# A streaming encoder layer on one core: buffers, lags, the queue of FFN weights, and the framework's scheduling model

## The chip, the cores and the metric

The kernel runs on one core of a Trainium2 chip. Time is device time in microseconds (us); lower is better. A core has a matrix engine (TensorE, in profiles PE, with its weight loads as PEld), a vector engine (VectorE, DVE), a scalar engine (ScalarE, ACT), a general one (GpSimd, POOL) and a queue engine (SyncE, SP), which here only issues DMA transfers. Each engine works through its own list of instructions in order; semaphores make one engine wait for another. SBUF is the on-chip memory, PSUM holds the results of matmuls, in 8 banks.

## The reference

One layer of a hybrid encoder over 2,048 prompt frames and 64 sample frames, width 1024. Shortened to what is computed:

```python
h = rms_norm(x, norm1_g) * (1 + sc1) + sh1            # sc, sh, gt: from silu(c) @ w_ada + b_ada
glu_a, glu_b, q, k, v, g_conv, g_attn = split(h @ w_in)
u = glu_a * sigmoid(glu_b)
conv_out = silu(layer_norm(depthwise_conv31(u))) @ w_conv_out
q, k = rms_norm per head (8 heads of 64)
o = softmax(q k^T / 8 + rel_bias, over own chunk of 64 and the 8 before) @ v
merged = sigmoid(g_conv) * conv_out + sigmoid(g_attn) * (o @ w_attn_out)
x = x + gt1 * (merged @ w_o)
h2 = rms_norm(x, norm2_g) * (1 + sc2) + sh2
gate, up = split(h2 @ w_ffn_in)                        # 2 x 2816 columns
x = x + gt2 * ((silu(gate) * up) @ w_ffn_out)
```

The outputs are both `x`, the last convolution inputs, and the new rows of keys and values. All data is 32 bit.

## The kernel before

Each large product is made of three matmuls on split operands: a value is rounded to a high part, the rest is the low part, and `mm3` adds high x high, high x low and low x high. So each weight slab (128 x 1024) passes through a chain: a DMA brings the raw slab (tags `wst`, three buffers, `wup`, one, `wfo`, two), ACT copies it into `whi`, and POOL or DVE subtracts to make `wlo`. There are five buffers (`held`) of each. A slab that is used again is written to DRAM already split (`w_d..._h`, `_l`) and later read back by DMA alone.

The work has two stages. In the first (to about 1210 us of the profile), four blocks of some 512 frames (`PBLOCKS`) are normalised, turned to columns, and multiplied with the input projection. Beside that run the depthwise convolution on DVE (480 instructions), the layer norm, and attention by head. For a head, `load_qk` fetches `q2` and `kk` (one buffer each, four DMAs on SP); four score tiles `sc` (one buffer of two PSUM banks) go to DVE and ACT for the softmax (`pr`), are transposed by TensorE (`ptp`), split (`ph`, `pl`) and multiplied with `vv` (`po`). In the second stage, three blocks (`CBLOCKS`) each run the merge (`ps<-cin`), the output projection (`pw`), the residual with second norm and transposes (`residual`), and the FFN. The FFN uses a Strassen-like scheme on halves of the frames (operands `t1` to `t4`, `b11` to `b22`, weight sums `ws` made on POOL), and `down` multiplies pairs of hidden tiles with `w_ffn_out` (`pd`). The last `down` of a block takes four tiles at once.

The order of the work comes from two layers. The kernel's own planner, class `Stream`, keeps an estimated load of each engine, and decides while the code is emitted when a step of a lane (attention, convolution, norms, residual turns) comes up between matmuls; its lags are constants such as `TURN_LAG`, `DMA_LAG`, and its prices are in `Stream.add`. Class `Weights` decides when raw slabs are loaded, split and freed. After that the framework's scheduler (`tile.TileContext`) simulates the emitted program, puts the instructions of each engine in a final order, gives out the buffers and sets the semaphores.

The profile names line 99 for nearly all instructions, because each goes through `Meter.run`; it is read by tile names instead. The lines the change touches: `last_phase` and `free_tag` (the raw buffers a kind may use), `split` (which engine makes `wlo`), `available` (whether the next slab may be split), `first_rows`, `store_v` and `norm_tile` (the buffers of `x`), `qk_rows` (the lag before key transposes), `down` (when it takes its weights), and the call of `TileContext`.

Of the kernel before, what the change touches and what calls it, by code (L numbers as in the profile page):

```python
# [16 lines left out]
P = 128  # L17
# [25 lines left out]
TT_LESS = 9e9  # L43
PE_LAG = 400.0
TURN_LAG = 2500.0
ON_ACT = (3,)
ON_POOL = ()
DMA_LAG = 4000.0
# [108 lines left out]
class Stream:  # L157
# [7 lines left out]
    def add(self, name, op, n, args, kw):  # L165
        if name == "pe":
            x = args[1]
            if op == "transpose":
                ns = 128 / 1.2
            elif x.dtype == F32:  # L170
                ns = max(n, 64) / (2.4 if "tile_position" in kw else 0.6)
            else:
                ns = (n if n >= 256 else 512) / 2.4
        elif name == "act":
            ns = 220 + 0.83 * n
        elif name == "pool":
            ns = 180.0 * n if ALU.pow in args else 60 + 2.25 * n
        else:
            fast = op in ("tensor_scalar", "tensor_copy")
            ns = 75 + n * (8.3 if op == "reciprocal" else 0.75 if fast else 1.04)  # L180
        self.load[name] = max(self.load[name], self.load["pe"]) + ns
# [66 lines left out]
class Weights:  # L248
# [5 lines left out]
    def __init__(self, engines, pool, dram, stream, keys, source, staging, held, kept):  # L254
        self.stream = stream
        self.sync, self.act, self.dve, self.gps = engines
        self.pool, self.dram, self.keys, self.source = pool, dram, keys, source
        self.staging, self.held = staging, held
        self.sum_pool, self.sum_d, self.sums, self.hold, self.landed = None, None, {}, 0, {}
        self.room, self.leaving = {"wst": staging, "wup": 0, "wfo": 0}, {"wst": 0, "wup": 0, "wfo": 0}  # L260
        times, raws = {}, {}
        self.items, self.users, self.need, self.first, self.stored = [], [], {}, set(), {}

        def item(key):
            self.items.append(key)
            self.users.append(0)
            return len(self.items) - 1

        for i, key in enumerate(keys):
            n = times[key] = times.get(key, 0) + 1  # L270
            if key[0] == "up" and n == 1:
                self.first.add(i)
                cs = [c for f, op in key[1:] for c in self.columns_of(f, op)]
                for c in cs:
                    if c not in raws:
                        raws[c] = item(("fi", c))
                self.need[i] = sorted({raws[c] for c in cs})
                for f, op in key[1:]:
                    for c in self.parts_of(f, op):
                        self.users[raws[c]] += 1  # L280
            elif n == 1 or not kept(key):
                self.need[i] = [item(key)]
                self.users[self.need[i][0]] += 1
        self.raws = raws
        self.again = {key for key, n in times.items() if n > 1 and kept(key)}
        self.loaded, self.ready, self.used, self.freed, self.given = {}, [], 0, 0, 0

        self.extra = {"wup": 1, "wfo": 2}
        self.tags = {"fo": ("wfo",), "": ("wst", "wup")}
        self.due = {kind: [] for kind in self.tags}  # L290
        for i, key in enumerate(self.items):
            self.due[self.kind(key)].append(i)
        self.load_on("")
# [12 lines left out]

    def last_phase(self, sum_pool, sum_d):
        self.sum_pool, self.sum_d = sum_pool, sum_d
        for kind, tag in (("fo", "wfo"), ("", "wup")):
            self.room[tag] = self.extra[tag]  # L310
            self.load_on(kind)

    @staticmethod
    def kind(key):
# [1 line left out]

    def free_tag(self, kind, sure=True):

        return next((t for t in self.tags[kind] if self.room[t] + (0 if sure else self.leaving[t]) > 0), None)

    def load(self, kind, sure=True):
        tag = self.free_tag(kind, sure)
        i = self.due[kind].pop(0)
        srcs, a, b = self.source(self.items[i])
        pool, bufs = (self.pool, self.staging) if tag == "wst" else (self.sum_pool, self.extra[tag])
        st = pool.tile([P, a, b], F32, tag=tag, name=tag, bufs=bufs)
        for j, src in enumerate(srcs):
            self.sync.dma_start(st[:, j * a // len(srcs) : (j + 1) * a // len(srcs)], src)
        self.loaded[i] = st, tag
        self.room[tag] -= 1  # L330
        self.landed[i] = self.stream.load["pe"] + DMA_LAG
        if self.items[i][0] == "fi":
            self.stream.at(self.landed[i], self.presum, True)
        self.fill()

    def load_on(self, kind):
# [3 lines left out]
    def drop(self, j, name):  # L340

        self.users[j] -= 1
        if self.users[j]:
            return
        _, tag = self.loaded.pop(j)
        self.leaving[tag] += 1

        def left():
            self.leaving[tag] -= 1
            self.room[tag] += 1  # L350
            self.load_on(self.kind(self.items[j]))

        self.stream.at(self.stream.when(name), left, True)

    def operand(self, f, op):
# [6 lines left out]
        while len(made) < int(op[1]):  # L362
# [5 lines left out]
            )[j]()  # L368
            self.gps.tensor_tensor(t, x, y, e)
            made.append(t)  # L370
            for c in self.parts_of(f, f"s{j + 1}"):
                self.drop(self.raws[c], "pool")
            self.stream.at(
# [12 lines left out]
    def split(self):  # L386
# [10 lines left out]
        if not its:  # L397
            for t, d in zip((hi, lo), self.stored[key][0]):
                self.sync.dma_start(t.bitcast(F32), d)
            return  # L400
        e, name = (self.dve, "dve") if key[0] in ("in", "qkv") or key[0] == "wo" and key[1] % 2 else (self.gps, "pool")
        if i in self.first:
            parts = [(slice(4 * j, 4 * j + 4), self.operand(f, op)) for j, (f, op) in enumerate(key[1:])]
            self.stream.after("act", "pool")
# [25 lines left out]
    def available(self):  # L430
        i = len(self.ready)
        if i >= len(self.keys):
            return False
        if i in self.need:
            return self.there(i) and not (self.hold and self.keys[i][0] == "up")
        return self.keys[i] in self.stored

    def fill(self):
# [75 lines left out]
def streaming_layer(ctx: ExitStack, tc: tile.TileContext, I, O):  # L514
# [271 lines left out]
        yield  # L786

    def first_rows():
        places = ((wa, "x", 2), (wa, "x", 2), (wa, "vst", 1), (wk, "kk", 1), (wk, "q2", 1))
        return [load_x(*tl, *place) for tl, place in zip(token_tiles(*PBLOCKS[0]), places)]  # L790

    def first_block(xs):
# [99 lines left out]
        stream.at(stream.when("act", "dve"), store)  # L892

    def store_v(src, n, row):
        vst = wa.tile([P, 4, 4, HD], F32R, tag="vst", name="vst", bufs=1)
        s = src[:n].rearrange("p (a c d) -> p a c d", a=4, c=2)
        stream.after("act", "pe")
        act.activation(vst[:n, :, 0:4:3], s, AF.Copy)
        stream.after("dve", "act")
        dve.tensor_tensor(vst[:n, :, 1:3], s, vst[:n, :, 0:4:3].bitcast(F32), ALU.subtract)  # L900
        stream.at(stream.when("act", "dve"), lambda: nc.sync.dma_start(
            v_d[row : row + n].rearrange("t h d -> t (h d)"), vst[:n].rearrange("p a c d -> p (a c d)").bitcast(F32)
        ))

    def qk_rows(ps, n, g, dst, col, out_rows):
# [14 lines left out]
        if out_rows is not None:  # L920
# [1 line left out]
            e, name = either(512, TT_LESS)  # L922
            e.tensor_tensor(ko[:n], kn[:n], gk[:n].unsqueeze(1).to_broadcast([n, NH, HD]), ALU.mult)
            stream.at(stream.when(name), lambda: nc.sync.dma_start(out_rows, ko[:n].rearrange("p h d -> p (h d)")))
        yield t + TURN_LAG
        store_kq(kn.rearrange("p h d -> p (h d)"), n, dst, col, g)

    def v_rows(ps, n, t):
# [68 lines left out]
    def norm_tile(lo, t, free):  # L997

        c = slice(t - lo, t - lo + P)
        x_t = load_x(t, P, wa, "x", 2)  # L1000
        yield stream.load["pe"] + DMA_LAG
        r = square(x_t, P)
        yield stream.when("pool")
        dve.tensor_scalar(x_t, x_t, r, None, ALU.mult)
# [478 lines left out]
    turns = Lane({}, TURN_NS, wide=2)  # L1483
    stream.lanes = [turns, work]

    def drain():
        turns.drain()
        work.drain()

    W.last_phase(wk, sum_d)  # L1490

    def gt_row(w, which):
        t = quarter(f"gt{which}", 1, F32, (P, D))
# [122 lines left out]
    c0, c1 = tile_chunks(*CBLOCKS[0])  # L1616
    nxt = [first_gates, gate_columns(*c0, 1)]
    srcs = [src]
    for s, (lo, hi) in enumerate(CBLOCKS):
        tiles = token_tiles(lo, hi)  # L1620
        half = (hi - lo) // 2
# [159 lines left out]
            dve.tensor_tensor(y, y, v, ALU.mult)  # L1781
            late.append((f, 1, y))

        def down(fs):

            last = fs[-1] == NF - 1
            ws = [W.get(("fo", f)) for f in fs]
            for i, (t, n) in enumerate(tiles):
                c = slice(t - lo, t - lo + n)
                if fs[0] == 0:  # L1790
# [55 lines left out]
            turns.step(turns.gens[0])  # L1846
        W.hold = False
        W.presum()
        turns.drain()
        for step, f in ((first, 3), (first, 4), (second, 2), (second, 3), (second, 4)):  # L1850
            step(f)
            W.fill()
        for f in range(0, NF, 2):
            ops = Operands(f)
            if f // 2 % 2 and f >= NF - 4:
                hid[1] = wk.tile([P, 2, 2, CW], F32R, tag="m1", name="hid")
            up(f, ops, lambda: down([f - 2, f - 1]) if 2 <= f <= NF - 4 else None)
            up(f + 1, ops, lambda: None)
        hidden(*late.pop())
        drain()  # L1860
        gt2 = {which: gt_row(1, which) for which in {int(t < SMP) for t, _ in tiles}}
        x1s = [quarter("x1", 1, F32, (P, 3, 512)) for _ in range(4)]
        for i, (t, n) in enumerate(tiles):
# [3 lines left out]
        if s + 1 < len(CBLOCKS):  # L1867
            nxt = [gate_columns(*tile_chunks(*CBLOCKS[s + 1])[0], ct) for ct in range(2)]
            srcs = [load_mixed(*c, i) for i, c in enumerate(tile_chunks(*CBLOCKS[s + 1]))]
        down(list(range(NF - 4, NF)))  # L1870
        stream.flush()


# [27 lines left out]
```

## Time and profile before

| | us |
|---|---|
| median of 3 runs | 3077.89 (3075.58 to 3080.13) |
| profiled execution | 3072.38 |
| its span | 3070.6 |
| TensorE busy | 2960.8 (96%) |
| VectorE busy | 1781.8 (58%) |
| ScalarE busy | 1179.6 (38%) |
| GpSimd busy | 1027.6 (33%) |
| mean granted TensorE clock | 0.986 |
| data moved | 676.27 MB, 220 GB/s |

A row of a group names engine, operation, output<-inputs (buffer numbers left out) and count, then busy time and the mean duration of one in ns, then the idle time of the engine before them and what ended it. A row of waits reads: who waited <- for what: us in total, times, longest. A row of the timeline has start and length in us, engine, operation and count; in brackets stands the idle time before it. "Landing" is the time from the issue of a DMA until its data has arrived. The granted clock is the share of its full rate that TensorE was allowed.

### The profile page before, as it was taken

How to read it: one execution, taken by the hardware profiler on the slowest of the kernel's cores; microseconds unless marked ns; L12 is line 12 of the kernel's file. 1: busy time of each engine (PE TensorE's matmuls, PEld its weight loads, DVE VectorE, ACT ScalarE, POOL GpSimd, SP SyncE). 2: the span in 40 equal slices, each digit the busy share in tenths (PEclk: the TensorE clock that was granted, in tenths of full speed). 3: DMA queues.
4: the chain of work that ended last, by engine and by line, in shares of the span. 5: the costliest groups of instructions: out<-in, count | busy, mean ns of one | idle time of the engine just before them, and what ended most of it. 6: DMA issues, size and time to landing. Idle time of an engine off the chain costs nothing. (4 is left out here: it accounts for less than half of the span.)

```text
span 3070.6 us, 44482 instructions
## 1 busy us (share of the span) xinstructions
PE 2960.8 (96%) x16403; PEld 2634.3 (86%) x16403; DVE 1781.8 (58%) x3435; ACT 1179.6 (38%) x2110; POOL 1027.6 (33%) x642
## 2 busy tenths in 40 slices
PE   7899898999999999999999989999999999999999
PEld 4789776887888888898999977889999999999998
DVE  5798688677877885454444335554444556344345
ACT  3334431452254357354333332453333244322321
POOL 0201210111011102448777854344445343343331
PEclk9999999999999999999999999999999999999999
DMA  9789788887887788876455567654444965334434
GB/s 344 247 298 303 226 296 282 272 268 266 281 270 238 275 273 253 262 246 229 150 169 172 192 222 244 224 185 153 151 151 134 342 213 194 126 117 131 138 110 161
DMA packets 480167, 676.27 MB, mean 220 GB/s; under 512 B 37716, under 2 KB 316104, under 8 KB 479949
## 3 DMA queue, kind: packets, MB, share of 16 engines
q1 hardware_dynamic: 467669, 656.04, 65.2%
q10 hardware_dynamic: 12280, 17.39, 1.6%
q8 instruction: 129, 2.11, 0.3%
q14 instruction: 89, 0.73, 0.1%
HBM read 501.70 MB, written 171.61 MB: 219 GB/s over the span
## 5 line engine op out<-in xcount | busy, mean ns | idle before, releaser
L99 POOL TENSOR_TENSOR wlo<-wst,whi 128x1024 fp32r<-128x1024 f32 (+1 forms) x215 | 458.7, 2142 | 607.8 <-ACT whi L99 555.6
L99 PE MATMUL ps<-t,whi 128*128 128x352 f32 (+2 forms) x2112 | 510.4, 325 | 8.3 <-DVE t L99 3.8
L99 PE MATMUL pd<-whi,hid 128*128 128x512 f32 (+1 forms) x1496 | 467.9, 391 | 16.4 <-ACT whi L99 16.4
L99 ACT ACTIVATE whi<-wst 128x1024 fp32r<-128x1024 f32 (+1 forms) x268 | 258.9, 975 | 433.2 <-PE pd L99 180.8
L99 PE MATMUL ps<-b,whi 128*128 128x352 f32 (+2 forms) x1584 | 381.4, 324 | 2.9 <-ACT early L99 1.8
L99 PEld LDWEIGHTS ps<-t,whi 128*128 128x128 f32 x2112 | 371.1, 189 | 13.9 <-DVE t L99 5.0
L99 DVE SCALAR_TENSOR_TENSOR y<-u,wd,y 128x512 f32<-128x512 f32 (+1 forms) x480 | 369.9, 774 | 6.8
L99 PE MATMUL ps<-hh,whi 128*128 128x512 f32 (+2 forms) x992 | 364.9, 368 | 0.0
L99 PE MATMUL ps<-hl,whi 128*128 128x512 f32 (+2 forms) x992 | 347.8, 351 | 0.0
L99 PE MATMUL ps<-hh,wlo 128*128 128x512 f32 (+2 forms) x992 | 347.4, 350 | 0.0
L99 PEld LDWEIGHTS pd<-whi,hid 128*128 128x128 f32 (+1 forms) x1496 | 276.7, 185 | 79.9 <-ACT whi L99 16.8
L99 PE MATMUL ps<-t,wlo 128*128 128x352 f32 (+2 forms) x1056 | 341.9, 324 | 0.1
L99 DVE TENSOR_TENSOR acc<-acc,pd 128x512 f32<-128x512 f32 (+1 forms) x272 | 187.0, 688 | 207.5 <-PE pd L99 207.5
L99 PE MATMUL pd<-wlo,hid 128*128 128x512 f32 (+1 forms) x748 | 292.5, 391 | 2.2 <-POOL wlo L99 1.3
L99 PEld LDWEIGHTS ps<-b,whi 128*128 128x128 f32 x1584 | 276.1, 188 | 4.8 <-ACT early L99 2.7
L99 PE MATMUL ps<-b,wlo 128*128 128x352 f32 (+2 forms) x792 | 256.2, 324 | 0.0
L99 POOL TENSOR_TENSOR r<-t,mhalf 128x1 f32<-128x1 f32 (+3 forms) x68 | 83.7, 1233 | 408.9 <-DVE t L99 389.4
L99 PEld LDWEIGHTS ps<-hh,wlo 128*128 128x128 f32 x992 | 188.7, 190 | 23.5 <-issue 0.5
L99 PEld LDWEIGHTS ps<-hh,whi 128*128 128x128 f32 x992 | 189.9, 191 | 18.8 <-issue 2.5
L99 PEld LDWEIGHTS ps<-hl,whi 128*128 128x128 f32 x992 | 189.8, 191 | 15.8 <-issue 1.7
L99 PEld LDWEIGHTS ps<-t,wlo 128*128 128x128 f32 x1056 | 200.3, 190 | 0.4 <-POOL wlo L99 0.4
L99 POOL TENSOR_TENSOR wlo<-wup,whi 128x1024 fp32r<-128x1024 f32 (+1 forms) x69 | 146.0, 2116 | 149.2 <-ACT whi L99 128.8
(206 smaller groups left out, 5431.8 us busy)
## 6 DMA issues: line engine op xcount, KB each, us to landing
whi<-w_din_h SPq DMA_DIRECT2D x72, 512.0 KB, 6.2
wlo<-w_din_l SPq DMA_DIRECT2D x72, 512.0 KB, 6.6
wst<-sum_d SPq DMA_DIRECT2D x132, 256.0 KB, 2.9
wmod<-in_w_ada SPq DMA_DIRECT2D x48, 512.0 KB, 8.8
sum_d<-ws SPq DMA_DIRECT2D x88, 256.0 KB, 4.8
whi<-w_dfo_h SPq DMA_DIRECT2D x44, 512.0 KB, 5.3
wlo<-w_dfo_l SPq DMA_DIRECT2D x44, 512.0 KB, 6.5
wst<-in_w_ffn_in SPq DMA_DIRECT2D x84, 256.0 KB, 3.3
```

The lines of the kernel that those rows point to most:

```text
L99: return f(*args, **kw)
```

## The change

It has three parts: some lags, prices and buffers; the raw buffers and the queue of FFN weights; and the flag of the framework's scheduler. With the flag, the scheduler simulates the program with another timing model of the framework, its timeline model, and orders each engine's instructions by that.

```diff
+KN_LAG = 5000.0
+X_LAG = 8000.0
...
-            ns = 180.0 * n if ALU.pow in args else 60 + 2.25 * n
+            ns = 260.0 * n if ALU.pow in args else 60 + 2.25 * n
...
-        self.tags = {"fo": ("wfo",), "": ("wst", "wup")}
+        self.tags = {"fo": ("wfo", "wup", "wst"), "": ("wst", "wup")}
...
     def last_phase(self, sum_pool, sum_d):
         self.sum_pool, self.sum_d = sum_pool, sum_d
-        for kind, tag in (("fo", "wfo"), ("", "wup")):
-            self.room[tag] = self.extra[tag]
-            self.load_on(kind)
+        self.open("", "wup")
+
+    def open(self, kind, tag):
+        self.room[tag] = self.extra[tag]
+        self.load_on(kind)
...
-        return next((t for t in self.tags[kind] if self.room[t] + (0 if sure else self.leaving[t]) > 0), None)
+        tags = self.tags[kind]
+        if kind == "fo" and any(self.items[i][0] == "fi" for i in self.due[""]):
+            tags = tags[:1]
+        return next((t for t in tags if self.room[t] + (0 if sure else self.leaving[t]) > 0), None)
...
         if self.items[i][0] == "fi":
             self.stream.at(self.landed[i], self.presum, True)
+            self.stream.at(self.landed[i], self.fill, True)
...
-        e, name = (self.dve, "dve") if key[0] in ("in", "qkv") or key[0] == "wo" and key[1] % 2 else (self.gps, "pool")
+        e, name = (self.dve, "dve") if i >= 4 and key[0] in ("in", "qkv") or key[0] == "wo" and key[1] % 2 else (self.gps, "pool")
...
         if i in self.need:
-            return self.there(i) and not (self.hold and self.keys[i][0] == "up")
+            now = self.stream.load["pe"]
+            if not self.there(i) or self.hold and self.keys[i][0] == "up":
+                return False
+            if i not in self.first or not self.careful():
+                return True
+            return all(self.landed[j] <= now for j in self.need[i]) and all(
+                self.made.get((f, int(op[1]) - 1), 1e18) <= now for f, op in self.keys[i][1:] if op[0] == "s"
+            )
...
-        places = ((wa, "x", 2), (wa, "x", 2), (wa, "vst", 1), (wk, "kk", 1), (wk, "q2", 1))
+        places = ((wa, "x", 3), (wa, "x", 3), (wa, "x", 3), (wk, "kk", 1), (wk, "q2", 1))
...
-        vst = wa.tile([P, 4, 4, HD], F32R, tag="vst", name="vst", bufs=1)
+        vst = wa.tile([P, 4, 4, HD], F32R, tag="x", name="vst", bufs=3)
...
-        yield t + TURN_LAG
+        yield t + KN_LAG
...
-        x_t = load_x(t, P, wa, "x", 2)
-        yield stream.load["pe"] + DMA_LAG
+        x_t = load_x(t, P, wa, "x", 3)
+        yield stream.load["pe"] + X_LAG
...
+    W.careful = lambda: bool(turns.gens)
...
-    W.last_phase(wk, sum_d)
...
     srcs = [src]
+    W.last_phase(wk, sum_d)
...
-        def down(fs):
+        def down(fs, ws):
             last = fs[-1] == NF - 1
-            ws = [W.get(("fo", f)) for f in fs]
...
         W.presum()
+        if not s:
+            W.open("fo", "wfo")
         turns.drain()
...
         drain()
+        ws = [W.get(("fo", f)) for f in range(NF - 4, NF)]
         gt2 = {which: gt_row(1, which) for which in {int(t < SMP) for t, _ in tiles}}
...
-        down(list(range(NF - 4, NF)))
+        down(list(range(NF - 4, NF)), ws)
...
-    with tile.TileContext(nc) as tc:
+    with tile.TileContext(nc, schedule_with_timeline_sim=True) as tc:
```

The weights of the last `down` of a block are now taken before the rows that its residual needs are requested. `made` holds the planner's time of each weight sum, which `careful` reads while residual turns are pending.

More of the change, by code (lines that the diff above doesn't have):

```diff
@@ L259, in __init__ @@
         self.sum_pool, self.sum_d, self.sums, self.hold, self.landed = None, None, {}, 0, {}
+        self.made, self.careful = {}, lambda: False
         self.room, self.leaving = {"wst": staging, "wup": 0, "wfo": 0}, {"wst": 0, "wup": 0, "wfo": 0}
@@ L350, in left @@
             self.room[tag] += 1
-            self.load_on(self.kind(self.items[j]))
+            for kind in self.tags:
+                self.load_on(kind)
         self.stream.at(self.stream.when(name), left, True)
@@ L370, in operand @@
             made.append(t)
+            self.made[f, j] = self.stream.when("pool")
+            self.stream.at(self.made[f, j], self.fill, True)
             for c in self.parts_of(f, f"s{j + 1}"):
@@ L1856, in streaming_layer @@
                 hid[1] = wk.tile([P, 2, 2, CW], F32R, tag="m1", name="hid")
-            up(f, ops, lambda: down([f - 2, f - 1]) if 2 <= f <= NF - 4 else None)
+            up(f, ops, lambda: down([f - 2, f - 1], [W.get(("fo", e)) for e in (f - 2, f - 1)]) if 2 <= f <= NF - 4 else None)
             up(f + 1, ops, lambda: None)
```

## The prediction

> **What bounds the kernel now.** I read the page first, then the busy time by stretch, then TensorE's own waits, and last the instructions around the longest of them.
>
> ```profile
> span 3070.6 us, 44482 instructions
> PE 2960.8 (96%) x16403; PEld 2634.3 (86%) x16403; DVE 1781.8 (58%) x3435; ACT 1179.6 (38%) x2110; POOL 1027.6 (33%) x642
> ...
> 0.00:150.00 150.00, 121.53 (x699) 91.19 (x700) 95.75 (x184) 49.91 (x84) 24.68 (x30) 0.95 0.86 294
> 150.00:1205.00 1055.00, 1017.98 (x5726) 865.20 (x5725) 834.33 (x1758) 441.05 (x874) 121.60 (x115) 0.98 0.85 274
> 1205.00:1800.00 595.00, 581.01 (x3169) 529.39 (x3169) 263.13 (x471) 249.00 (x452) 398.06 (x283) 0.99 0.59 196
> 1800.00:1875.00 75.00, 57.33 (x283) 48.77 (x282) 31.20 (x52) 13.98 (x22) 19.61 (x12) 0.89 0.81 277
> 1875.00:2400.00 525.00, 517.78 (x3073) 483.10 (x3071) 238.10 (x442) 204.85 (x335) 232.18 (x102) 1.00 0.55 180
> 2400.00:3070.00 670.00, 665.20 (x3462) 616.66 (x3460) 319.24 (x531) 220.81 (x345) 231.46 (x102) 1.00 0.50 166
> ```
>
> The columns are the stretch, its length, busy time of PE, PEld, DVE, ACT and POOL, then granted clock, DMA share and GB/s. TensorE is the bound everywhere: it idles 3070.6 - 2960.8 = 110 us, of which 28 in the first 150 us, 37 in the projections and attention (150 to 1205), 14 from there to 1800, 18 in the next 75 us, and 7 and 5 in the two later stretches. The FFN loop itself has nothing to give:
>
> ```profile
> 1425.00:1500.00 75.00, 75.00 (x412) 68.46 (x411) 28.60 (x51) 30.30 (x55) 55.40 (x41) 1.00 0.53 180
> ...
> 2337.16 13.62 PE pd L99 x60
> 2350.78 42.40 PE ps L99 x288
> ```
>
> The first row is a full 75 us of 75; the chain of waits gives 42.40/288 = 147 ns for a 320-wide and 13.62/60 = 227 ns for a 512-wide matmul. With these prices the matmuls of a stretch of program order can be turned into time; I call that the cover between two instructions. TensorE's waits:
>
> ```profile
> PE pd L99 <- ACT whi L99: 16.4, 1, 16.4
> PE pt L99 <- DVE kn L99: 11.2, 3, 5.0
> PE sc L99 <- DVE sm L99: 9.9, 7, 5.8
> PE ps L99 <- DVE t L99: 9.9, 5, 6.1
> PE ptp L99 <- DVE pr L99: 7.5, 8, 2.9
> PE pt L99 <- DVE x_t L99: 5.2, 6, 1.5
> PE sc L99 <- DMA kk<-k_d: 4.9, 3, 3.5
> ...
> PE ps L99 <- ACT t L99: 3.3, 4, 1.4
> ...
> PE po L99 <- ACT ph L99: 1.2, 2, 0.7
> ```
>
> **Part 1: the FFN output weights (`tags`, `free_tag`, `open`, `ws` taken ahead of `down`).** The 16.4 us wait is a transfer stuck in SP's queue:
>
> ```profile
> 1813.03 1.06 ACT L99 ACTIVATE whi<-wfo 128x1024 fp32r<-128x1024 f32 x1
> 1814.80 10.07 SPq L1866 DMA_DIRECT2D x<-x_d  x12
> 1834.66 1.73 SPq L328 DMA_DIRECT2D wfo<-in_w_ffn_out  x1
> 1845.67 1.06 ACT L99 ACTIVATE whi<-wfo 128x1024 fp32r<-128x1024 f32 x1 [21.27 <-DMA wfo<-in_w_ffn_out]
> 1846.78 1.12 PE L99 MATMUL pd<-whi,hid 128*64 128x512 f32 x2 [16.35 <-ACT whi L99]
> ```
>
> With two `wfo` buffers the last raw slab could go out only behind twelve `x1` reads, the gates and the mixed columns of the next block. In the built program after the change, both last raw slabs (now in a `wst` and the `wup` buffer) stand before the `x_t` reads of the next block, well ahead of the twelve. The wait and the 1.3 us that POOL's half adds go: -18. What is late next are the `w_conv_out` slabs whose buffers they borrowed: two of four now stand ahead of the jump, the others behind it; the last `down` of that block covers them with 33 us (144 matmuls of 227 ns), so I cost that at 0; without the cover it is one landing, 3 to 5 us.
>
> **Part 2: lags, buffers and queues.** KN_LAG doubles a planner delay between the key norm and its transposes; the cover from product to transposes rises from a median of 10.5 us to 13.9, but the shortest, near 1 and 8 us, stay short. Of 11.2 us I take -3 (0 to -11). X_LAG and the third `x` buffer: -3 of 5.2. `vst` shares that ring of three, so a store of `v` can hold an `x` load; three buffers hold what three held before (two and one): 0. The `i >= 4` test moves four weight halves to POOL:
>
> ```profile
> L99 POOL TENSOR_TENSOR wlo<-wst,whi 128x1024 fp32r<-128x1024 f32 (+1 forms) x215 | 458.7, 2142 | 607.8 <-ACT whi L99 555.6
> L99 DVE TENSOR_TENSOR wlo<-wst,whi 128x1024 fp32r<-128x1024 f32 x53 | 66.1, 1253 | 46.7 <-ACT whi L99 43.5 <-DMA q_d<-part_l 2.7 <-issue 0.2
> L99 ACT ACTIVATE whi<-wst 128x1024 fp32r<-128x1024 f32 (+1 forms) x268 | 258.9, 975 | 433.2 <-PE pd L99 180.8
> ```
>
> That is 4 x (2142 - 1253) ns = 3.6 us slower, but POOL has 25 us of work in the first 150 and DVE 96: 0 (between +4 and -4). `careful` and the extra `fill` calls keep weight splits out of ACT's and POOL's way while the residual turns end; it aims at the `t` waits, 9.9 + 3.3 us, of which 6.1 is at the first merge and not touched: -5, with a further -3 for the later `last_phase`, which takes its first loads out of the jam there.
>
> **Part 3: the schedule.** This moves more than all the rest. Against the order in which the kernel's code emits them, 1,954 of some 16,170 TensorE instructions stand elsewhere in the program before, 11,240 in the program after; the matmuls are the same. With the flag alone removed from the changed kernel it would be 2,163. What counts is cover, which I read off the built order. The key and query tiles `kk` and `q2` have one buffer each: a head's load can start only when the head before it has issued its last score matmul. Cover from that matmul to the next head's first score, in us, for the eight heads of the last block:
>
> ```
> before  23.8  14.1   8.2   7.8   7.9   8.6  11.0   8.2
> after   25.2   1.8   1.4   4.8   5.7   1.9   1.0   3.9
> ```
>
> In the new order the four score tiles of a head stand some 5 us apart instead of 2, and the next head follows at once. What such a load needs, from the trace:
>
> ```profile
> 1088.28 0.74 PE L99 MATMUL sc<-kk,q 128*128 128x320 f32 x4
> 1089.05 0.61 SPq L1229 DMA_DIRECT2D q<-q_d  x1
> ...
> 1091.00 0.60 SPq L1230 DMA_DIRECT2D kk<-k_d  x1
> DMA to landing us min/median/max: 4.3/5.3/7.7
> ```
>
> The landing row is for the `kk` loads of 1040 to 1200 us. From the end of the score (1088.9) to the last issue are 2.1 us, plus 5.3: 7.4 us, 6.4 to 9.8 at the ends. Before, the shortest of the 24 covers of blocks 1 to 3 is 7.8, so the loads are just hidden, which the 4.9 us of `kk` waits confirm. After, the shortfalls to 7.4 add up to 9 + 7 + 31 = 47 us (32 at a need of 6.4; 95 at 9.8), and the smaller tiles of block 0 add about 8. Other waits between the two points lengthen the real cover, so I take +40 (15 to 60). [...]
>
> ```profile
> 1241.89 0.90 PE L99 MATMUL ps<-cin,whi 128*128 128x320 f32 x2 [6.10 <-DVE t L99]
> ...
> 1242.86 0.73 PE L99 MATMUL ps<-cin,whi 128*128 128x320 f32 x2
> ...
> 1243.66 0.73 PE L99 MATMUL ps<-cin,whi 128*128 128x320 f32 x2
> ...
> 1245.16 0.46 PE L99 MATMUL ps<-cin,whi 128*128 128x320 f32 x2
> ...
> 1245.60 0.46 PE L99 MATMUL ps<-cin,whi 128*128 128x320 f32 x2
> ```
>
> Three matmuls take 0.80 us right after the stall (1242.86 to 1243.66) and 0.44 once it is over (1245.16 to 1245.60): in the 3 us between, some 1.5 us are lost. Seven shortfalls are near 3 us or more: +8 (0 to 15).
>
> The other chains of the front: score to transposed probabilities (`pr`) has a lower quarter of its covers at 6.6 instead of 7.3 us, and the shortest fall from 1.2 to 0.4; the split halves `ph` go from 2.9 to 1.6. If all waits of 7.5 and 1.2 us doubled it would be +9; tripled, +17. I take +10, because part falls into the same gaps (0 to 30). The score bank gets more cover (median 2.7 to 4.9), but its shortest ones, which make the 9.9 us, stay: 0. The first products of an FFN block (`b11`) come 2 us after the last transposes instead of 5: +5 for two blocks (0 to 10), while `t3` gets more cover (some 9 to 13 us), whose gain is counted in part 2.
>
> In the FFN loop the new order eats slack: the shortest time from the last use of a weight buffer to the first use of its next tenant falls from 12.2 to 4.5 us for `whi` and from 12.4 to 6.2 for `wlo`. Refilling takes 975 ns on ACT and then 2142 on POOL (rows above), 3.1 us, so both still hold. The stored slabs of blocks 2 and 3 fall to 7.1 us:
>
> ```profile
> whi<-w_dfo_h SPq DMA_DIRECT2D x44, 512.0 KB, 5.3
> wlo<-w_dfo_l SPq DMA_DIRECT2D x44, 512.0 KB, 6.5
> ```
>
> 5.3 us and 6.5 (whose slack is 8.3) just fit: +2 (0 to 40, below).
>
> [...]
>
> **Sum.** +40 +8 +10 +5 +2 = +65; -18 -3 -3 -8 = -32; together +33. The profiled execution took 3072.38 us (span 3070.6) and would be 3105; it lies 5.5 under the median of the runs, 3077.89, so the runs come to 3111, which I give as 3110.
>
> **Rivals.**
> - *Faster.* The short covers were counted as if TensorE ran through between two heads. If the waits on `pr`, `ph` and the score bank already lie there, the load lands meanwhile and `kk` costs under 15 us with no clock loss; the point where it decides is a `kk` term of 15 (10 + 5 + 2 = 17 of other losses, against gains of 32). With `kk` at 5 and `pr` at 0 the sum is 5 + 7 - 32 = -20, and with KN_LAG's full 11 us it is -28: 3078 - 28 = 3050. For it: DVE has 834 us of work in 1055 there, so waits on it do abound. Against it: in the last block eight heads follow each other with nearly nothing between. Chance 0.23.
> - *About even.* The loads land sooner than the row says, with less traffic while TensorE stalls: the shortfalls fall to a third, the `kk` term from 40 to 13, and the sum to 33 - 27 = +6, or less where the clock holds: 3078 to 3084; the trace's least landing of 4.3 speaks against it. Chance 0.08, of which 0.05 within 0.2%.
> - *Much slower: the FFN loop loses its cover.* If SP stands behind another transfer when a stored slab's buffer comes free, each of the 20 or so pairs of blocks 2 and 3 costs 2 us more: +40 on the sum, 3150. For it: SP's queue is in order, and the 16.4 us wait shows what that does. Against: the loop's row above has no idle time at all, and its DMA share is 0.53. Chance 0.11.
> - *As forecast:* 0.58.
>
> The range: below, the faster case's 3050 less a few us; above, 3110 with the `kk` and `pr` terms at their upper ends (20 + 20) and something of the FFN case: 3044 to 3165. The likeliest case's own range is 3085 to 3145. A measurement of this kernel tells about 0.2% (6 us) from no change. Slower 0.58 + 0.11 + 0.03 = 0.72, same 0.05, faster 0.23.
>
> **What the next profile shows.** The wait of `pd` on ACT must be gone from 1800 us. The waits `sc <- DMA kk` must rise from 4.9 to 40 or so, most of them between 1040 and 1210 us, with dips of the granted clock there; waits on `pr` above 15 us. The FFN stretches must still show 75 of 75. The forecast is wrong if `kk` waits stay under 15 us, or if idle time appears in the FFN loop.

## The result, and the profile after

The changed kernel took 3158.74 us (median of 4 runs, 3158.06 to 3162.32), against 3078.80 us for the kernel before on the same chip: a ratio of 1.0264, 95% interval 1.0246 to 1.0281. It is 80 us slower; the forecast was slower by 32. The first fence has two lines of the page of the changed kernel; the second its busy time by stretch, in the same stretches and columns as in the prediction.

```profile
span 3156.5 us, 44573 instructions
...
PE 3000.4 (95%) x16403; PEld 2657.5 (84%) x16403; DVE 1775.6 (56%) x3431; ACT 1168.8 (37%) x2110; POOL 1038.0 (33%) x646
```

```profile
0.00:150.00 150.00, 122.56 (x697) 92.81 (x698) 89.39 (x176) 50.39 (x84) 34.49 (x32) 0.94 0.87 300
150.00:1205.00 1055.00, 978.54 (x5366) 826.00 (x5363) 799.65 (x1666) 384.80 (x787) 111.13 (x108) 0.96 0.78 257
1205.00:1800.00 595.00, 563.78 (x3016) 504.21 (x3017) 269.97 (x503) 264.05 (x471) 337.92 (x237) 0.97 0.60 198
1800.00:1875.00 75.00, 75.00 (x407) 67.89 (x406) 30.81 (x52) 25.91 (x51) 52.82 (x41) 1.00 0.49 164
1875.00:2400.00 525.00, 520.77 (x3044) 483.47 (x3043) 247.26 (x456) 200.18 (x333) 239.01 (x114) 1.00 0.60 201
2400.00:3157.00 757.00, 739.71 (x3881) 683.12 (x3879) 338.52 (x581) 243.45 (x389) 262.59 (x116) 0.99 0.49 164
```

The count of matmuls is the same, 16,403. So the 85.9 us of span (3156.5 against 3070.6) split into two parts without a rest: TensorE's busy time grew from 2960.8 to 3000.4, +39.6, and its idle time from 109.8 to 156.1, +46.3. Nearly half of the loss is the same matmuls taking longer.

The place is the front, the stage of projections and attention. Cut at the first merge matmul (`ps<-cin`, 1223 us before, 1322 after), the same view gives for the kernel before:

```profile
0.00:1223.00 1223.00, 1156.26 (x6511) 970.33 (x6511) 939.47 (x1962) 504.97 (x980) 153.47 (x148) 0.98 0.84 274
```

and for the changed kernel:

```profile
0.00:1322.00 1322.00, 1197.14 (x6511) 997.89 (x6511) 942.98 (x1958) 500.36 (x980) 166.17 (x152) 0.95 0.77 254
1322.00:3157.00 1835.00, 1803.22 (x9892) 1659.63 (x9892) 832.61 (x1474) 668.41 (x1130) 871.79 (x494) 0.99 0.55 185
```

The same 6,511 matmuls: the front is 99 us longer, 58 of it idle (66.7 to 124.9) and 41 busy time, with the granted clock at 0.95 instead of 0.98. Everything behind the cut is 13 us shorter. TensorE's waits in the changed kernel:

```profile
PE sc L101 <- DMA kk<-k_d: 34.7, 13, 5.8
PE ptp L101 <- DVE pr L101: 15.9, 5, 4.1
PE ptp L101 <- ACT pr L101: 12.9, 8, 4.6
PE pa L101 <- DVE ssq L101: 7.4, 1, 7.4
PE ps L101 <- ACT hh L101: 7.1, 5, 2.3
PE pd L101 <- DVE acc L101: 6.1, 3, 3.0
PE pd L101 <- DMA whi<-w_dfo_h: 5.7, 2, 3.7
PE ps L101 <- ACT b L101: 5.3, 2, 3.1
```

The 16.4 us of `pd` on ACT is gone, the `kk` load leads with 34.7 instead of 4.9, and the two waits on `pr` are 28.8 instead of 7.5. Where a head waits for its keys, the chain of waits of the changed kernel shows the mechanism step by step:

```profile
1232.04 0.61 PE sc L101 x4
1232.65 0.02 issue
1232.66 0.61 SPq L1249
1233.27 0.04 issue
1233.33 0.03 issue
1233.36 0.56 SPq L1250
1233.92 0.05 issue
1233.97 0.60 SPq L1249
1234.57 0.05 issue
1234.62 5.10 DMA kk<-k_d
1239.72 0.14 issue
1239.86 1.41 PE sc L101 x4
```

The last score of a head ends at 1232.65, its four loads are issued (`q2` at line 1249, `kk` at 1250), the last lands 5.10 us later, and the next head's first score starts at 1239.86: 7.2 us, where the prediction had 7.4. What a stall does to the clock stands in the timeline of the changed kernel, at a smaller one:

```profile
1206.54 1.33 PE L101 MATMUL ptp<-ident,pr 128*128 128x128 f32 x5 [2.36 <-ACT pr L101]
...
1209.44 0.63 PE L101 MATMUL ps<-hh,whi 128*128 128x512 f32 x1
1209.87 0.63 PE L101 MATMUL ps<-hl,whi 128*128 128x512 f32 x1
...
1213.21 0.39 PE L101 MATMUL ps<-hh,whi 128*128 128x512 f32 x1
1213.44 0.40 PE L101 MATMUL ps<-hl,whi 128*128 128x512 f32 x1
```

After 2.36 us of idling, 512-wide matmuls stand 0.43 us apart (1209.44 to 1209.87), and 0.23 only from 1213.2 on; the trace's record of the granted clock stands at 0.5 for 6.8 us from 1206.3. It has 14 such spells before, 90 us in all (51 of them in the front), and 27 after, 150 us (130 in the front). Part of a spell is idle time and costs nothing more. TensorE was busy in them for 60 us before and 120 after (39 and 105 in the front), and half of that is time lost. So the clock makes 30 of the 39.6 us of added busy time, and 33 of the 41 in the front; the other 8 to 10 us are not assigned here.

### The profile page after: what moved, and what is told of

Same layout as the page of the kernel before. It is cut to its first block, busy times and chain, and to the rows that moved or that the text cites. A ratio compares the mean times of both kernels' runs of the same rounds, so it can differ in the third digit from the quotient of the medians.

```text
span 3156.5 us, 44573 instructions
## 1 busy us (share of the span) xinstructions
PE 3000.4 (95%) x16403; PEld 2657.5 (84%) x16403; DVE 1775.6 (56%) x3431; ACT 1168.8 (37%) x2110; POOL 1038.0 (33%) x646
## 4 chain that ended last, share of the span: by engine, by line
PE 85%; DMA 6%; DVE 5%; ACT 2%; issue 1%; SPq 1%; ACTq 0%; POOL 0%; DVEq 0%; POOLq 0%
PE ps L101 55%; PE pd L101 16%; PE pw L101 6%; PE po L101 2%; DMA kk<-k_d 2%; PE sc L101 2%; PE ptp L101 1%; DVE y L101 1%; PE pt L101 1%; PE pa L101 1%; DMA tg<-g_d 1%; DVE pr L101 1%; DVE h L101 0%; DMA wlo<-w_dqkv_l 0%; DMA x<-x_d 0%
## 5 line engine op out<-in xcount | busy, mean ns | idle before, releaser
L101 PE MATMUL pd<-whi,hid 128*128 128x512 f32 (+1 forms) x1496 | 490.0, 394 | 11.8 <-DVE acc L101 6.1
L101 POOL TENSOR_TENSOR r<-t,mhalf 128x8 f32<-128x8 f32 (+3 forms) x68 | 86.4, 1277 | 409.6 <-DVE t L101 390.2
L101 POOL TENSOR_TENSOR wlo<-wup,whi 128x1024 fp32r<-128x1024 f32 (+1 forms) x73 | 158.1, 2166 | 186.4 <-ACT whi L101 162.0
L101 ACT ACTIVATE pr<-pr,sm 128x640 f32<-128x640 f32 (+5 forms) x168 | 128.2, 764 | 217.7 <-DVE sm L101 212.9
```

The source lines that it names most:

```text
L101: return f(*args, **kw)
```

## The experiments

All ratios are to the kernel before, run on the same chip in the same series; 0.1% is 3 us. Times of two series are compared only roughly.

**The flag taken away, and the flag alone.** Two kernels that split the change in two:

```diff
-    with tile.TileContext(nc, schedule_with_timeline_sim=True) as tc:
+    with tile.TileContext(nc) as tc:
```

> The changed kernel with the timeline-model schedule taken away and everything else kept. Theory T (the new order of the instructions makes the loss, buffers and queues gain): about 3050 us (3040 to 3060), waits of `sc` on the `kk` load near 5 us, no wait of `pd` on ACT near 1800 us, first `ps<-cin` matmul near 1210 to 1225 us after the span's start. Rival R1 (the longer lags and the shared buffers make the loss in the front): 3120 to 3160 us, first `ps<-cin` matmul near 1300 us.

Measured: 3056.40 us, ratio 0.9919 (0.9902 to 0.9936), 26 us faster than before. Two rows of its waits and one of its stretches:

```profile
PE ptp L101 <- DVE pr L101: 9.8, 6, 5.8
...
PE sc L101 <- DMA kk<-k_d: 7.6, 4, 3.0
```

```profile
0.00:1235.00 1235.00, 1162.62 (x6511) 973.49 (x6511) 935.62 (x1958) 505.40 (x980) 168.78 (x152) 0.98 0.84 272
```

The reverse edit, the same flag set in the kernel before:

> The kernel before with the timeline-model schedule alone. Theory T: 3165 to 3185 us, the front 90 to 110 us longer than before, the 16 us wait of `pd` near 1800 us (or one like it) still there, 25 to 40 us of waits of `sc` on the `kk` load. Rival R1: about 3078 us, with `kk` waits near 5 us.

Measured: 3171.60 us, ratio 1.0293 (1.0277 to 1.0308). The first merge matmul comes at 1318 us, 94 later than before; its `kk` waits are 38.2 us, and a wait of `pd` on ACT of 11.4 us is there. Theory T holds in both: the flag is the loss, 102 us on top of the new buffers and queues (3158.7 against 3056.4, from two series) and 89 on the old ones, and the rest of the change gains 26. The lags and shared buffers (R1) don't make the front 100 us longer; but it isn't shorter either, as T had it (1210 to 1225 us): the first merge matmul comes at 1236 us without the flag, 12 later than before.

**TensorE held in emitted order.** With the flag on, TensorE's instructions of the front are each tied behind the one before:

```diff
+            if self.name == "pe" and self.stream.pin:
+                self.stream.pin(out)        # tc.keep_in_program_order, front only
```

> The changed kernel with the timeline-model schedule, but TensorE's instructions of the front (projections and attention, up to the merge) held in the order in which the code emits them; the other engines stay free in order. Theory T (the loss comes from TensorE's order): 3060 to 3085 us. Rival R2 (the order of the DMA queue, VectorE and ScalarE makes it): 3110 us or more, with `kk` waits of 25 us or more although TensorE's order is the emitted one.

Measured: 3160.27 us, ratio 1.0252 (1.0231 to 1.0274): no better than with TensorE free, and the `kk` waits are the largest row by far.

```profile
PE sc L101 <- DMA kk<-k_d: 51.0, 14, 9.2
PE pa L101 <- DMA wmod<-in_w_ada: 17.0, 10, 7.8
PE ptp L101 <- DVE pr L101: 13.1, 10, 4.1
```

So T in this form, that TensorE's order makes the loss and the emitted order would be free of it, fell. The time and the `kk` waits are those of R2, but they don't show its cause: the emitted order of TensorE can itself be short of cover, which the next runs bear on. Holding TensorE in the feed-forward part too:

> As the run before it, with TensorE's instructions held in emitted order in the feed-forward part too. If the new order there costs or gains nothing (as forecast, +2), within 6 us of the run that holds the front alone; if the feed-forward part lost cover, 10 to 40 us less; if its new order gains, more.

Measured: 3181.20 us, ratio 1.0324 (1.0309 to 1.0339), 21 us more than with the front alone: the flag's order of the feed-forward part is better than the emitted one. The ordinary schedule's is better still: from the first merge matmul to the end it takes 1819 us without the flag and 1834 with it.

**Which queue, or all of them.** The same tie for the DMA issues of SP alone, and for all engines and SP:

> The changed kernel with the timeline-model schedule, with only the DMA issues of SP held in the emitted order in the front. If the order of the loads makes the loss: 3080 to 3110 us. If the loss sits in TensorE, VectorE and ScalarE: 3150 us or more, with `kk` waits near 35 us as before.

Measured: 3186.84 us, ratio 1.0350 (1.0332 to 1.0368); `kk` waits 32.4 us. Holding the loads in emitted order brings nothing back; it costs 28 us more (two series).

> The changed kernel with the timeline-model schedule, but with the instructions of all engines and of the DMA queue held in the front in the order in which the code emits them. Theory T3 (the timeline model's order of the engines and queues beside TensorE made the loss that holding TensorE alone did not undo): front (to the first `ps<-cin` matmul) near 1235 us, time near 3060 us. Rival R3 (the emitted order is no better in itself; the ordinary scheduler gets its gain by the small moves that it makes, some 1,750 of 6,278 TensorE and 1,575 of 1,825 VectorE instructions of the front): front 1290 to 1330 us, time 3120 to 3165 us.

Measured: 3281.47 us, ratio 1.0660 (1.0641 to 1.0678), the slowest of all. The first merge matmul comes at 1442 us. T3 falls. The direction of R3 holds, far past its numbers (front 1290 to 1330 us, time 3120 to 3165):

```profile
PE sc L101 <- DMA kk<-k_d: 96.6, 16, 15.2
PE pa L101 <- DVE R L101: 16.8, 1, 16.8
PE sc L101 <- DVE sm L101: 15.1, 19, 2.0
```

The built orders say why for a part of it. For the heads that follow each other closest, the emitted order has 4.3 to 4.8 us of matmuls between two heads, about the 4.0 us that the planner's own lag puts there. The ordinary scheduler makes 7.8 to 8.6 of them, just above the 7.2 us that a load takes; the timeline model makes 1.0 to 5.7 in the last block. The traces agree: between two heads of the last block stand at the closest 17 to 22 matmuls with all engines held, 43 to 47 in the ordinary schedule, and 9 to 33 in that of the timeline model.

The other part is the queue. Of the 96.6 us, 51.8 are four waits at the first head of a block (15.2, 9.3, 13.6 and 13.7). Ahead of the last three stand 93 to 415 matmuls, so their cover isn't short; there the first `kk` load was issued 22 to 81 us after the last score of the head before, behind other transfers of a queue held in emitted order. With TensorE alone held, 50 of the 51.0 us come at 17 to 41 matmuls, so those are waits of cover.

The ordinary schedule is thus no copy of the emitted one. Its moves (some 1,750 of 6,278 TensorE instructions of the front) are worth 206 us in this stage (first merge matmul at 1236 us instead of 1442), and the timeline model's only 120 (1322).

**A second buffer for keys and queries.** It fits only if the modulation weights go from four buffers to two, so there is a control with that alone.

```diff
-        q2 = wk.tile([P, 2, QB], F32R, tag="q2", name="q2", bufs=1)
-        kk = wk.tile([P, 1024], F32R, tag="kk", name="kk", bufs=1)
+        q2 = wk.tile([P, 2, QB], F32R, tag="q2", name="q2", bufs=2)
+        kk = wk.tile([P, 1024], F32R, tag="kk", name="kk", bufs=2)
...
-    M = Slabs(nc.sync, wa, stream, list(mod_order()), source, 4)
+    M = Slabs(nc.sync, wa, stream, list(mod_order()), source, 2)
```

> Control for the next run: the changed kernel with two instead of four buffers for the modulation weights. Within 15 us of 3159 us, most of it from waits of `pa` on `wmod`.

> As the control, with the room used for a second buffer of `kk` and `q2` each, so that a head's load no longer waits for the head before. Waits of `sc` on `kk` fall from 35 us or more to under 5. Theory T2 (that wait and the half-clock time behind it make most of the loss of the front): 50 to 80 us under the control. Rival R4 (other waits take its place, on `pr` and `sm`, since the heads then follow each other closer): under 20 us.

Measured: control 3204.07 us, ratio 1.0420 (1.0398 to 1.0442), three times dearer than expected, with 24.1 us of waits on `wmod` and the `kk` waits up to 51.6; with the second buffer 3155.41, ratio 1.0253 (1.0237 to 1.0270). The second buffer is worth 49 us, a shade under T2's 50 to 80. The waits in the kernel with it:

```profile
PE sc L101 <- DVE sm L101: 23.8, 12, 3.9
PE pa L101 <- DMA wmod<-in_w_ada: 23.8, 10, 7.4
PE ps L101 <- ACT hh L101: 11.5, 6, 2.6
PE sc L101 <- DMA kk<-k_d: 8.3, 4, 5.0
```

`kk` falls from 51.6 (control) to 8.3, not under 5, and the next head's score now waits for the score bank instead: `sm` rises from 1.6 in the control's front to 23.8. Then the same buffers under the ordinary schedule:

> The ordinary schedule with the same buffers as the second-buffer run: two for `kk` and `q2` each, two for the modulation weights. It says how much of the timeline-model schedule's loss (102 us) is left when no head waits for the head before. Theory T2 (the `kk` load with its clock time is most of the loss): 3100 to 3130 us, so that the two schedules are then 25 to 55 us apart. Rival R5 (the loss lies as much in the other chains, the score tiles and probabilities, and the feed-forward part): 3060 to 3085 us, 70 to 95 us apart.

Measured: 3069.95 us, ratio 0.9974 (0.9963 to 0.9985). With these buffers in both, the two schedules are still 85 us apart, against 102 without (the control's two modulation buffers alone were not run under the ordinary schedule). R5's numbers came: the `kk` load is the largest single wait, but with it relieved, most of the loss shows up elsewhere. Part of these 85 us is new, though: waits on the modulation weights are 23.8 us with the flag and 12.3 without, where the changed kernel had 1.2. How much of the flag's own loss the second buffer takes away is therefore not shown.

**The planner's lag.** The lag between a head's load and its scores, 9.0 instead of 4.0 us, in both schedules:

```diff
-            loaded[i] = stream.load["pe"] + DMA_LAG
+            loaded[i] = stream.load["pe"] + 9000.0
```

> The ordinary schedule with everything else of the change kept, and the planner's lag between the load of a head and its scores raised from 4.0 to 9.0 us. In the built order the shortfalls of the `kk` cover to 7.4 us then sum to 5 us instead of 10. If the 7.6 us of `kk` waits and their half-clock time are all there is to win: 3044 to 3052 us, against 3056. If the longer lag starves TensorE elsewhere: 3056 to 3075 us.

> The changed kernel with its timeline-model schedule and the same 9.0 us lag. If that schedule follows the order in which the planner emits, the `kk` waits fall under 15 us and the time to about 3110 us. If it makes its own order and takes no account of the lag (built order: shortfalls to 7.4 us of 53 us instead of 47 for the last 24 heads), `kk` waits stay at 30 to 45 us and the time within 20 us of 3159.

Measured: ordinary schedule 3061.03 us, ratio 0.9949 (0.9933 to 0.9965), not better than 3056.40, as the second expectation had it: `kk` falls from 7.6 to 2.7 us, and `sm` takes it over with 23.4 (8.9 before the edit). With the flag 3163.45, ratio 1.0271 (1.0248 to 1.0294), `kk` waits 35.3: that schedule doesn't follow the lag.

**Part 1 alone,** on the kernel before: `tags`, `free_tag`, `open`, the other kind's loads in `left`, and `ws` taken ahead of `down`.

> The kernel before with the first part of the change alone: the feed-forward output weights may use the `wst` and `wup` buffers, and the last four of a block are asked for ahead of the twelve `x1` reads. The prediction's term: -18 us (3060), the 16 us wait of `pd` near 1800 us gone, nothing else moved. If a removed stall also takes its half-clock time with it: -22 to -28 us (3050 to 3056). If the borrowed buffers hold up the next block's columns: 0 to -10 us.

Measured: 3051.75 us, ratio 0.9911 (0.9896 to 0.9925), 27 us faster, with an interval that overlaps that of the whole change without its flag (0.9902 to 0.9936). No kernel tried here was faster. Its page, and the stretch that had the 16.4 us wait (57.33 of 75 us busy before, clock 0.89):

```profile
span 3049.4 us, 44485 instructions
...
PE 2956.7 (97%) x16403; PEld 2631.8 (86%) x16403; DVE 1783.9 (59%) x3435; ACT 1179.3 (39%) x2110; POOL 1029.2 (34%) x642
```

```profile
1800.00:1875.00 75.00, 73.47 (x435) 66.07 (x434) 43.84 (x78) 21.48 (x34) 34.24 (x17) 1.00 1.00 330
```

Between the profiles, idle time falls by 17.1 us (109.8 to 92.7) and busy time by 4.1 (2960.8 to 2956.7): the stall took its slow matmuls with it. Against the medians the gain is 27; the profiled execution of before was 5.5 us under its own median.

## Why the prediction was right and wrong

The direction, the place (`kk` loads between two heads of the front) and the cause (the schedule) held. That the time lies in the range is luck: it is above the likeliest case's own 3085 to 3145, where the range had been left open for the `kk` and `pr` terms at their upper ends and for the FFN loop, and `kk` came below its middle and the loop kept its cover. The sum was 33 and came to 86 in the profiles. Of the 53 missing, 22 are the clock (30 instead of 8), 21 idle time, and 10 the busy time that isn't assigned.

- *The clock term, +8 (0 to 15)*: this is the step that failed, by the largest amount: it measures 30. I counted only stalls of near 3 us or more, seven of them; no run shows such a limit, so none shows the term that I made with it either. Where the clock is on record (from 30 us on), every gap of 3 us and more does lie at a spell of half clock, 7 in the kernel before and 12 in the changed one. But of the 22 spells in the front of the changed kernel only nine begin at such a gap; the other 13 begin at gaps of 1.5 to 2.7 us, like the one shown. In the front, 58 us of added idle time came with 33 us lost to the clock and 41 of busy time in all, where I had put 8 on 57.
- *`kk` waits, +40 (15 to 60)*: they rose by 29.8, to 34.7. The need was right (7.2 measured, 7.4 forecast) and the shortfalls of the built order, 47 + 8, were the right upper bound; 15 taken off for other waits in the same gaps was too little by 10.
- *`pr` and `ph`, +10 (0 to 30)*: the waits on `pr` rose by 21.3, and together with those of `ptp` on `sm` by 25.6. The direction was right, and with `sm` the size lies in the term's range; the waits on `pr` more than tripled.
- *`b11`, +5*: the new wait of `ps` on ACT's `b` is 5.3. *Stored slabs, +2*: `pd` on `w_dfo_h` is 5.7, in two waits. The loop itself keeps its cover (75.00 of 75 us from 1800 to 1875), so the rival in which it loses it fell.
- *Costed at nothing*: the 7.4 us on `ssq`, 5.4 more on `hh` and 6.1 on `acc` had no term. I looked for lost cover only in chains that I had priced, and these had shown little or no wait before. These 19 us and the 16 more on `pr` and `sm` outweigh the 10 less on `kk`.
- *Part 1, -18*: it is -27 by itself in the medians and -21 between the profiles. The wait went as forecast, and 4 us of slow matmuls with it, which I had left out on this side too.
- *KN_LAG, X_LAG, `careful`: -14 together*: without the flag the whole change is worth 26 and part 1 alone 27, so these are about 0, some 7 us either way by the intervals. In the run without the flag, the wait of `pt` on `kn` did fall from 11.2 to 3.1, but TensorE's idle time in the front rose, from 66.7 us to 72.4.
- *"With the flag alone removed"*: my measure for what the flag does, how many instructions stand away from the emitted order, was misleading. The emitted order in the front, with none moved, is the slowest schedule of all. What had to be compared was the cover, which I did for `kk`, and it gave the place but not the sum. (The first number of each row of covers is not the distance between two heads: in the traces that is 69 us before and 72 after. No shortfall hangs on it.)
- *The faster rival (0.23)* needed a `kk` term under 15; it is 30. Waits on `pr` do lie in such gaps, as it said (one of 1.54 us stands in the last fence of this document), but they covered only part of the load.

What stays open: why the timeline model spaces heads and tiles so. No run changed its own durations, so it isn't shown which of them is off. Nor did a run change the clock alone; that 30 us of the busy time are the clock rests on the equal counts of matmuls, the record of spells and the spacing of 0.43 against 0.23 us.

## What to carry to other kernels

Price a stall of TensorE with what follows it: here a microsecond of new idle time in the front cost 1.7, and gaps from some 1.5 us on were enough for it. When a scheduler's model is exchanged, don't price the one chain that looks shortest: with that chain freed, the two schedules were still 85 us apart (102 before), on other chains. And in a change of several parts, build each alone: the edits of the FFN weights' queue held the whole gain, 27 us, and the flag beside it hid that under nearly four times as much.

## What the runs showed of the hardware

Spells of half clock came in steps of 3.4 us: 3.4, 6.8, 13.7 or 17.1 long in the kernel before, 3.4, 6.8 or 10.2 in the changed one, apart from the ends of the runs. Not every spell followed a long gap. In the timeline of the changed kernel a spell begins at 1237.0 us, when TensorE had idled 1.54 and 0.36 us:

```profile
1235.76 0.66 PE L101 MATMUL ptp<-ident,pr 128*128 128x128 f32 x4 [1.54 <-ACT pr L101]
1236.78 0.62 PE L101 MATMUL po<-ph,vv 128*128 128x512 f32 x1 [0.36 <-ACT ph L101]
1239.86 1.41 PE L101 MATMUL sc<-kk,q 128*128 128x320 f32 x4 [2.46 <-DMA kk<-k_d]
```

In the 3.4 us ahead of each of the 22 spells in the front, TensorE's gaps sum to 1.7 to 3.4 us, so that half of that time was enough. The reverse held there too. In each of these two profiles, all spells lie on one grid of 3.413 us; of the other full-clock windows of that grid in the front of the changed kernel, 308 from 66 us on, none has more than 1.4 us of gaps (1.1 in the kernel before). So in this front the sum of the gaps in a window told whether a spell followed, not the length of one gap. Behind the front the line is less sharp: in the kernel before, a spell at 2019.9 us follows 1.4 us, and windows with 1.6 and 1.7 (from 1381.6 and 1828.7 us) are followed by none.

The profiles give the landing time of few `kk` loads in the last block: 4.0 and 5.4 us for two after, 4.3 to 7.7 for four before. Whether it fell, as the rival with less traffic had it, isn't shown by so few.
